# The products with w_down in three column pieces of 342, 342 and 340 instead of two of 512

## The chip, the core and the metric

The kernel runs on one core of a Trainium2 chip. The metric is the time of one execution in microseconds (us); three runs of the kernel before gave 2617.18, 2617.27 and 2620.52, so the median is 2617.27 us. A trace of one further execution of the same kernel goes with them. Its engines are TensorE (PE: matmuls; PEld: the loads of the stationary operand, which the trace lists apart), VectorE (DVE), ScalarE (ACT), GpSimd (POOL) and SyncE (SP, which issues the DMAs).

## The reference, cut to what matters

Two transformer blocks follow one another on 1024 tokens of 1024 features, all in float32. The first mixes a gated delta rule with a dilated attention, the second a gated unit with a depthwise convolution of width 31. Each ends in a feed-forward stage, and only these two stages are touched. In them `x` is (1024, 1024), `D_FF` is 2816, and `w_ff2` has 4096 rows:

```
u = causal_dwconv(h @ w_up, ffn_conv_w)
gate, up = u[..., :D_FF], u[..., D_FF:]
x = x + (jax.nn.silu(gate) * up) @ w_down          # first block
...
f = jnp.square(jax.nn.relu(jnp.einsum('bsd,df->bsf', h, w_ff1[l])))
x = x + jnp.einsum('bsf,fd->bsd', f, w_ff2[l])      # second block
```

## The kernel before

Every product is made from float32 operands that are split in a high and a low part of a 4-byte format. `mm3` (L283) makes one product of a 128x128 stationary tile and a moving tile as three matmuls into the same accumulator: low by high, high by low, high by high. Each matmul has its own weight load. All of them go through `mm` and have line L281 in the profile.

`ffn` (L1545) makes a feed-forward stage. For each of its row blocks f of 128 hidden features (22 in the first block, 32 in the second) it makes the up products (tile `ps_up`, 512 columns), and after each second f it calls `down` for the two blocks before. `down` (L1563) goes over the 8 token tiles, and for each it runs `tile` (L1550): two halves of the 1024 output columns, each one PSUM tile `ps_dn` of 512 columns, into which 2 x 3 matmuls are added up (4 x 3 for the last four token tiles of a stage, where the last two pairs of f are taken together). The stationary operand is the hidden activations of the token tile (`g.hi`, `g.lo`), the moving operand is a slice of a row block of w_down (`w.hi`, `w.lo`, 1024 columns each in one buffer of 2048 words). After each half VectorE adds the PSUM tile to the residual `x[i]` (a tensor_tensor, L315, recorded by `evac`, L343). PSUM has 8 tiles of 512 columns (L357).

The order of all instructions is made on the host: `Weaver.run` (L137) keeps tasks with priorities and models when each engine becomes free (`cost`, L124). A matmul counts 0.417 ns a column there, a tensor_tensor 75 ns and 1.042 ns an element. The task that the model finds due issues its next step, and each engine then executes its own instructions in exactly that order. So a changed count of steps can change the order of work elsewhere.

After a token tile's last piece in the last `down` of the first stage, `last1` (L1749) normalises it, stores it and prepares it for the second block; when four tiles are through, `norm_half` (L549) transposes them (tile `ps_tr`). Then `in2` (L1865) begins: its products (`ps_vg`) feed a convolution of width 31 (`conv31`, L1801) over four groups of channels m = 0 to 3. It runs as chains of VectorE scalar_tensor_tensor steps (L327), 128x512 for m = 0 and 128x1024 for the others. Only for m = 3 the first three taps are matmuls (tile c31, shown as `ps_c`), which ScalarE brings into SBUF before VectorE goes on with that group. `conv_ln` (L1840) normalises each finished half group with two further PE steps (`ps_ct`, `ps_cb`). `block2` (L1915) has its products `ps_v` (256 columns) and `ps_u` in between, and the product `ps_out` of the second block waits for all of it. The second feed-forward stage ends the program: `last2` (L2052) normalises and stores each token tile.

Of the kernel before, what the change touches and what calls it, by code (L numbers as in the profile page):

```python
# [14 lines left out]
ALU = mybir.AluOpType  # L15
# [4 lines left out]
H = 512  # L20
D = 1024
# [52 lines left out]
def after(*evs):  # L74
    def cond():
        return max((e.t for e in evs), default=0.0) if all(e.done for e in evs) else -1.0
    return cond
# [181 lines left out]
class Prog(Weaver):  # L259
# [1285 lines left out]
    def ffn(self, x, h, hev, nf, np_, up, mid, tail, last):  # L1545

        G = {}
        self.gT = Ring([self.unit() for _ in range(2)])

        def tile(i, last_, todo):  # L1550
            kk = [(g, w) for ws, gs in todo for g, w in zip(gs, ws)]
            ts = slice(i * P, (i + 1) * P)
            for n in (0, H):
                ps = self.psum("dn")
                for q, (g, w) in enumerate(kk):
                    self.mm3(ps, g.hi[:, ts], g.lo[:, ts], w.hi[:, 0, n:n + H], w.lo[:, 0, n:n + H], q == 0, q == len(kk) - 1)
                e = self.evac("DVE", lambda xs=x[i][:, n:n + H], ps=ps: self.tt(xs, xs, ps, ALU.add))
                if n and last_:
                    last(i, after(e))
                self.hold = True  # L1560
                yield "PE"

        def down(*fs):  # L1563

            took = []
            for f0 in fs:
                ws = yield from self.pops(self.wq, 2)
                took.append((ws, [G.pop(f) for f in (f0, f0 + 1)]))
                gs = took[-1][1]
                yield "PE", after(*[g.ev[0] for g in gs])  # L1570
                if len(fs) == 1:
                    yield "PE", after(*[g.ev[1] for g in gs])
                if f0 == nf - 2:
                    tail()
                for i in range(4 if len(fs) > 1 else NT):
                    yield from tile(i, f0 == nf - 2, took[-1:])
            if len(fs) > 1:
                yield "PE", after(*[g.ev[1] for _, gs in took for g in gs])
                for i in range(4, NT):
                    yield from tile(i, True, took)  # L1580
            for ws, gs in took:
                for w in ws:
                    self.put(self.W, w)
                for g in gs:
                    self.put(self.gT, g.slot)
                    if len(fs) > 1:
                        s = yield from self.gT.get("PE")
                        s.buf.give()

        for f in range(nf):  # L1590
            G[f] = g = Slot(None)
            g.ev = [Ev(), Ev()]
        first = 2 // np_
        ws = yield from self.pops(self.wq, 2)
        for hf in range(2):
            yield "PE", after(*hev[hf])
            for q in range(2):
                f, p = q // np_, q % np_
                ps = self.psum("up")
                self.gemm_fm(ps, ws[q], 0, h[hf])  # L1600
                yield from up(f, p, hf, ps, G[f])
                if hf:
                    self.put(self.W, ws[q])
                self.hold = True
                yield "PE"
        for f in range(first, nf):
            g = G[f]
            if np_ == 2 and f == nf - 1:
                ws = yield from self.pops(self.wq, 2)
                for hf in range(2):  # L1610
                    for p, w in enumerate(ws):
                        ps = self.psum("up")
                        self.gemm_fm(ps, w, 0, h[hf])
                        yield from up(f, p, hf, ps, g)
                        if hf:
                            self.put(self.W, w)
                        self.hold = True
                        yield "PE"
                    for p in h[hf]:
                        p.give()  # L1620
                    if not hf:
                        for _ in range(2):
                            self.put(self.gT, self.unit())
                break
            for p in range(np_):
                w = yield from self.pop(self.wq)
                for hf in range(2):
                    ps = self.psum("up")
                    self.gemm_fm(ps, w, 0, h[hf])
                    yield from up(f, p, hf, ps, g)  # L1630
                    self.hold = True
                    yield "PE"
                self.put(self.W, w)
                if p == 0 and f % 2 == 0 and f < nf - 2:
                    yield from down(f - 2)
        else:
            for hb in h:
                for p in hb:
                    p.give()
                self.put(self.gT, self.unit())  # L1640
        mid()
        yield from down(nf - 4, nf - 2)
# [473 lines left out]
```

## Time and profile before

| | |
|---|---|
| median of three runs | 2617.27 us |
| profiled execution, time / span of its instructions | 2619.11 us / 2617.3 us |
| PE busy | 2540.3 us, 97% of the span |
| PE weight loads busy | 2180.4 us, 83% |
| VectorE / ScalarE busy | 1370.7 us, 52% / 807.9 us, 31% |
| mean granted clock of TensorE | 0.987 of 2.4 GHz |

A row of the list of groups reads: line, engine, operation, output tile <- inputs, shape, count, then busy time in us, mean ns of one instruction, and the idle time of the engine just before the group with what ended it. Matmuls overlap in the pipeline, so the mean duration of one (389 ns) is longer than the distance from one start to the next; that distance is read from a timeline, where a run of equal instructions stands in one row with its start, its length and its count. The difference of two rows' starts, divided by the count of the first, is the time that one of its matmuls takes from the sequence.

### The profile page before, as it was taken

What the parts mean: (1) busy time and instruction counts of PE and PEld (TensorE: products, weight loads), DVE (VectorE), ACT (ScalarE), POOL (GpSimd) and SP (SyncE); (2) the same over time, 40 slices, a digit from 0 to 9 for tenths busy, and PEclk for the clock granted to TensorE, in tenths of its full rate; (3) what the DMA queues carried; (4) which work ended last, traced back from release to release, by engine and by line L of the source; (5) the groups of instructions that cost most, each with busy time, mean ns of one, the idle gap of its engine ahead of it and who ended that gap; (6) DMA issues with size and microseconds to landing.
All of it is one profiled execution on the core that took longest, in us unless ns stands there. A gap on an engine that the chain in (4) does not pass through costs nothing.

```text
span 2617.3 us, 31361 instructions
## 1 busy us (share of the span) xinstructions
PE 2540.3 (97%) x13001; PEld 2180.4 (83%) x13001; DVE 1370.7 (52%) x1868; ACT 807.9 (31%) x1306; POOL 121.1 (5%) x245
## 2 busy tenths in 40 slices
PE   7999999988989999999999999989999999999998
PEld 6888999988978888888888888877788888888887
DVE  5441343454654555555555567969554444444444
ACT  5322443453541422222222235253232121212122
POOL 1010000000000000000000001050000000000000
PEclk9999999998989999999999999999999999999999
DMA  5232222232441111111111113102211111111111
GB/s 189 71 104 85 84 67 62 80 80 69 106 130 57 41 49 49 49 50 50 49 50 49 50 66 101 61 9 90 71 41 57 41 57 41 57 41 57 41 49 65
DMA packets 175164, 170.80 MB, mean 65 GB/s; under 512 B 25985, under 2 KB 148254, under 8 KB 175022
## 3 DMA queue, kind: packets, MB, share of 16 engines
q1 hardware_dynamic: 175022, 168.80, 21.2%
q8 instruction: 102, 1.67, 0.3%
q14 instruction: 40, 0.33, 0.0%
HBM read 145.50 MB, written 23.23 MB: 64 GB/s over the span
## 4 chain that ended last, share of the span: by engine, by line
PE 61%; issue 28%; DVE 4%; ACT 3%; DMA 2%; POOL 2%; SPq 0%; POOLq 0%; ACTq 0%; DVEq 0%
PE ps_up L281 18%; PE ps_dn L281 9%; PE ps_in L281 5%; PE ps_out L281 5%; PE ps_vg L281 3%; PE ps_dil L281 3%; PE ps_T L281 2%; ACT arF L311 2%; PE ps_S L281 2%; PE ps_z L281 2%; PE ps_O L281 2%; PE ps_dv L281 2%; DVE arF L327 2%; PE ps_pU L281 1%; PE ps_G L281 1%
## 5 line engine op out<-in xcount | busy, mean ns | idle before, releaser
L281 PE MATMUL ps_up<-arR 128*128 128x512 f32 x3648 | 831.5, 389 | 0.0
L281 PEld LDWEIGHTS ps_up<-arR 128*128 128x128 f32 x3648 | 684.5, 188 | 142.1
L315 DVE TENSOR_TENSOR arR<-arF,arR 128x1024 fp32r<-128x1024 f32 (+3 forms) x283 | 347.6, 1236 | 610.0 <-ACT arR L311 609.5
L281 PE MATMUL ps_dn<-arR 128*128 128x512 f32 x2592 | 591.8, 389 | 0.0
L311 ACT ACTIVATE arR<-arF 128x1024 fp32r<-128x1024 f32 (+3 forms) x297 | 311.2, 1071 | 852.3 <-PE ps_dn L281 394.3
L281 PEld LDWEIGHTS ps_dn<-arR 128*128 128x128 f32 x2592 | 486.4, 188 | 101.0
L315 DVE TENSOR_TENSOR arF<-arF,ps_dn 128x512 f32<-128x512 f32 x416 | 279.6, 684 | 183.2 <-PE ps_dn L281 183.2
L327 DVE SCALAR_TENSOR_TENSOR arF<-arF,pcol 128x1024 f32<-128x1024 f32 (+1 forms) x276 | 311.4, 1149 | 22.5 <-ACT arF L311 17.5
L311 ACT ACTIVATE arF<-arF 128x1024 f32<-128x1024 f32 (+3 forms) x158 | 134.8, 860 | 272.5 <-DVE arF L315 138.5
L281 PE MATMUL ps_out<-arR 128*128 128x512 f32 x768 | 182.2, 398 | 2.7 <-DVE arR L315 2.7
L281 PEld LDWEIGHTS ps_out<-arR 128*128 128x128 f32 x768 | 146.7, 192 | 34.4 <-DVE arR L315 3.7
L311 ACT ACTIVATE arF<-ps_up 128x512 f32<-128x512 f32 x152 | 89.5, 589 | 187.0 <-PE ps_up L281 187.0
L281 PE MATMUL ps_in<-arR 128*128 128x512 f32 x576 | 137.7, 399 | 0.0
L281 PEld LDWEIGHTS ps_in<-arR 128*128 128x128 f32 x576 | 109.4, 192 | 23.9
L315 DVE TENSOR_TENSOR arF<-arF 128x1024 f32<-128x1024 f32 (+4 forms) x91 | 89.1, 979 | 28.8 <-ACT arF L311 14.8
L281 PE MATMUL ps_dil<-arR 128*128 128x512 f32 x384 | 97.4, 403 | 0.0
L281 PE MATMUL ps_vg<-arR 128*128 128x512 f32 x384 | 88.3, 390 | 0.0
L281 PEld LDWEIGHTS ps_vg<-arR 128*128 128x128 f32 x384 | 71.8, 188 | 14.8
L281 PEld LDWEIGHTS ps_dil<-arR 128*128 128x128 f32 x384 | 71.7, 192 | 14.2
L281 PE MATMUL ps_O<-arF 128*128 128x128 f32 (+2 forms) x384 | 69.9, 328 | 12.2 <-ACT arF L311 6.8
L315 DVE TENSOR_TENSOR arF<-ps_G,csq 128x512 f32<-128x512 f32 x48 | 33.1, 690 | 90.8 <-PE ps_G L281 90.8
L315 DVE TENSOR_TENSOR arF<-arF,ps_out 128x512 f32<-128x512 f32 x64 | 43.5, 683 | 62.1 <-PE ps_out L281 62.1
(185 smaller groups left out, 2037.2 us busy)
## 6 DMA issues: line engine op xcount, KB each, us to landing
arF<-in_w_ff_dram SPq DMA_DIRECT2D x64, 512.0 KB
arF<-in_w_up_dram SPq DMA_DIRECT2D x44, 512.0 KB
arF<-in_w_in_dram SPq DMA_DIRECT2D x12, 1024.0 KB
arF<-in_w_down_dram SPq DMA_DIRECT2D x22, 512.0 KB
arF<-in_x_dram SPq DMA_DIRECT2D x16, 512.0 KB
arF<-in_w_out_dram SPq DMA_DIRECT2D x16, 512.0 KB
arF<-in_w_in_dram SPq DMA_DIRECT2D x16, 512.0 KB
arF<-kd SPq DMA_DIRECT2D x28, 256.0 KB
```

Of the source, the lines that this page charges most:

```text
L281: self.nc.tensor.matmul(out, lhsT, rhs, start=start, stop=stop, **kw)
L311: self.nc.scalar.activation(out, in_, func, **kw)
L315: self.nc.vector.tensor_tensor(out, a, b, op)
L327: self.nc.vector.scalar_tensor_tensor(out, a, s, b, op0, op1)
```

## The change

The two halves of 512 columns in `tile` become three pieces, columns 0 to 341, 342 to 683 and 684 to 1023. Each piece takes one PSUM tile, of which the first 342 or 340 columns are used, its own matmuls on the same stationary operands, and its own VectorE addition into `x`. The step that follows a token tile's last piece is issued after the third piece.

```
-            for n in (0, H):
-                ps = self.psum("dn")
+            for n, m in ((0, 342), (342, 684), (684, D)):
+                ps = self.psum("dn")[:, :m - n]
                 for q, (g, w) in enumerate(kk):
-                    self.mm3(ps, g.hi[:, ts], g.lo[:, ts], w.hi[:, 0, n:n + H], w.lo[:, 0, n:n + H], q == 0, q == len(kk) - 1)
-                e = self.evac("DVE", lambda xs=x[i][:, n:n + H], ps=ps: self.tt(xs, xs, ps, ALU.add))
-                if n and last_:
+                    self.mm3(ps, g.hi[:, ts], g.lo[:, ts], w.hi[:, 0, n:m], w.lo[:, 0, n:m], q == 0, q == len(kk) - 1)
+                e = self.evac("DVE", lambda xs=x[i][:, n:m], ps=ps: self.tt(xs, xs, ps, ALU.add))
+                if m == D and last_:
                     last(i, after(e))
```

The order of instructions is the same up to the first `ps_dn`. In both stages the row of 96 matmuls of 512 columns of a `down` becomes 144 of 342 and 340. At the end of the first stage the transposes move among the pieces too. On PE, from the end of the last `down` of the first stage, before:

```order
L281 MATMUL ps_dn<-arR 128x512 x168
L291 MATMUL ps_tr<-csq,arF 128x128 x32
L281 MATMUL ps_dn<-arR 128x512 x24
L281 MATMUL ps_vg<-arR 128x512 x72
L291 MATMUL ps_tr<-csq,arF 128x128 x32
L281 MATMUL ps_vg<-arR 128x512 x192
```

On PE at the same place, now (from the piece of the last token tiles on, where 12 matmuls make one piece):

```order
L281 MATMUL ps_dn<-arR 128x342 x24
L281 MATMUL ps_dn<-arR 128x340 x12
L281 MATMUL ps_dn<-arR 128x342 x12
L291 MATMUL ps_tr<-csq,arF 128x128 x32
L281 MATMUL ps_dn<-arR 128x342 x12
L281 MATMUL ps_dn<-arR 128x340 x12
L281 MATMUL ps_dn<-arR 128x342 x24
L281 MATMUL ps_dn<-arR 128x340 x12
L281 MATMUL ps_vg<-arR 128x512 x48
L291 MATMUL ps_tr<-csq,arF 128x128 x32
L281 MATMUL ps_vg<-arR 128x512 x168
```

The first 32 transposes now stand inside a token tile, and the second 32 have one product `ps_vg` of 24 matmuls fewer ahead of them.

On PE in `block2`, around the matmuls of the convolution's group m = 3 (`ps_c`), before:

```order
L281 MATMUL ps_v<-arR 128x256 x312
L281 MATMUL ps_ct<-csq,arF 128x128 x12
L281 MATMUL ps_c_11730<-arF 128x512 x3
L281 MATMUL ps_v<-arR 128x256 x24
L291 MATMUL ps_cb<-csq,arF 128x128 x4
L281 MATMUL ps_c_11795<-arF 128x512 x3
L291 MATMUL ps_cb<-csq,arF 128x128 x8
```

On PE at the same place, now:

```order
L281 MATMUL ps_v<-arR 128x256 x240
L281 MATMUL ps_ct<-csq,arF 128x128 x4
L281 MATMUL ps_v<-arR 128x256 x48
L291 MATMUL ps_cb<-csq,arF 128x128 x4
L281 MATMUL ps_ct<-csq,arF 128x128 x8
L281 MATMUL ps_v<-arR 128x256 x24
L281 MATMUL ps_c_12432<-arF 128x512 x3
L281 MATMUL ps_v<-arR 128x256 x24
L291 MATMUL ps_cb<-csq,arF 128x128 x8
L281 MATMUL ps_c_12502<-arF 128x512 x3
```

The second `ps_c` stands behind the same 336 matmuls of `ps_v` as before, but behind all twelve `ps_cb` instead of four.

On VectorE in the same stretch, from the first step of group m = 2, with the semaphores that a step waits for, before:

```order
L323 TENSOR_SCALAR arF<-arF,pcol 128x1024 [waits DVE_49,Pool_49]
L327 SCALAR_TENSOR_TENSOR arF<-arF,pcol 128x1024 [waits DVE_49] x12
L327 SCALAR_TENSOR_TENSOR arF<-arF,pcol 128x1024 [waits Activation_49,Pool_49]
L327 SCALAR_TENSOR_TENSOR arF<-arF,pcol 128x1024 [waits DVE_49] x3
L315 TENSOR_TENSOR arR<-arF,arR 128x1024 [waits DMAHW7_49,Activation_49]
```

On VectorE at the same place, now:

```order
L323 TENSOR_SCALAR arF<-arF,pcol 128x1024 [waits DVE_49,Pool_49]
L327 SCALAR_TENSOR_TENSOR arF<-arF,pcol 128x1024 [waits DVE_49] x18
L327 SCALAR_TENSOR_TENSOR arF<-arF,pcol 128x1024 [waits Activation_49,Pool_49]
L327 SCALAR_TENSOR_TENSOR arF<-arF,pcol 128x1024 [waits DVE_49] x3
L315 TENSOR_TENSOR arR<-arF,arR 128x1024 [waits DMAHW7_49,Activation_49]
```

The step that waits for ScalarE is the first tap of group m = 3 on VectorE; 18 taps of group m = 2 stand ahead of it instead of 12.

## Rows read from the trace of the kernel before

**Rows 1.** The page: busy time, share and instructions; clock in tenths, 40 slices.

```profile
PE 2540.3 (97%) x13001; PEld 2180.4 (83%) x13001; DVE 1370.7 (52%) x1868; ACT 807.9 (31%) x1306; POOL 121.1 (5%) x245
PEclk9999999998989999999999999999999999999999
```

**Rows 2.** Stretches: length, busy time by engine (instructions), granted clock, DMA share, GB/s.

```profile
920.00:1590.00 670.00, 670.00 (x2974) 555.34 (x2973) 371.21 (x409) 170.54 (x220) 13.57 (x63) 1.00 0.17 52
1590.00:1910.00 320.00, 304.31 (x1598) 258.63 (x1597) 245.59 (x280) 122.45 (x271) 51.89 (x71) 0.98 0.19 61
1910.00:2609.00 699.00, 699.00 (x3103) 579.30 (x3101) 328.23 (x391) 144.31 (x183) 6.73 (x18) 1.00 0.16 49
```

**Rows 3.** The costliest groups: busy us, mean ns | idle before, releaser.

```profile
L281 PE MATMUL ps_dn<-arR 128*128 128x512 f32 x2592 | 591.8, 389 | 0.0
L281 PEld LDWEIGHTS ps_dn<-arR 128*128 128x128 f32 x2592 | 486.4, 188 | 101.0
L281 PE MATMUL ps_G<-arF 128*128 128x128 f32 x384 | 50.9, 278 | 0.0
```

**Rows 4.** Timeline of PE, first down of stage one: start us, length us, instructions.

```profile
923.11 21.92 PE L281 MATMUL ps_dn<-arR 128*128 128x512 f32 x96
944.87 43.68 PE L281 MATMUL ps_up<-arR 128*128 128x512 f32 x192
988.39 21.92 PE L281 MATMUL ps_dn<-arR 128*128 128x512 f32 x96
```

**Rows 5.** Timeline of PE, a run of 256 columns and the row behind it.

```profile
1683.67 37.59 PE L281 MATMUL ps_v<-arR 128*128 128x256 f32 x312
1721.10 2.84 PE L281 MATMUL ps_ct<-csq,arF 128*128 128x128 f32 x24
```

**Rows 6.** Timeline of PE, a run of 260 columns and the row behind it.

```profile
177.10 46.14 PE L281 MATMUL ps_z<-arR 128*128 128x260 f32 x384
223.08 4.33 PE L281 MATMUL ps_dil<-arR 128*128 128x512 f32 x18
```

**Rows 7.** Timeline of PE, an early run of 512 columns and the row behind it.

```profile
129.08 16.88 PE L281 MATMUL ps_in<-arR 128*128 128x512 f32 x72
145.80 1.84 PE L281 MATMUL ps_ss<-ones,arF 128*128 128x1 f32 x16
```

**Rows 8.** Timeline of PE, a run of 128 columns in plain float32.

```profile
304.74 1.95 PE L281 MATMUL ps_G<-arF 128*128 128x128 f32 x16
```

**Rows 9.** VectorE groups that read PSUM, 512 and 256 columns.

```profile
L315 DVE TENSOR_TENSOR arF<-arF,ps_dn 128x512 f32<-128x512 f32 x416 | 279.6, 684 | 183.2 <-PE ps_dn L281 183.2
L315 DVE TENSOR_TENSOR arF<-ps_T,band 128x256 f32<-128x256 f32 x8 | 3.4, 424 | 4.7 <-PE ps_T L281 3.9 <-ACT arF L311 0.7
```

**Rows 10.** PE's waits between 1590 and 1910: us in total, times, longest.

```profile
PE ps_ct L281 <- DVE arF L327: 7.8, 2, 5.6
PE ps_c L281 <- ACT arF L311: 6.4, 1, 6.4
PE ps_out L281 <- DVE arR L315: 0.7, 1, 0.7
PE ps_cb L291 <- ACT arF L311: 0.5, 1, 0.5
PE ps_u L281 <- DVE arR L315: 0.4, 1, 0.4
```

**Rows 11.** Timeline of VectorE around the first tap of group m = 3.

```profile
1717.11 15.81 DVE L327 SCALAR_TENSOR_TENSOR arF<-arF,pcol 128x1024 f32<-128x1024 f32 x12
1750.41 4.87 DVE L327 SCALAR_TENSOR_TENSOR arF<-arF,pcol 128x1024 f32<-128x1024 f32 x4 [17.50 <-ACT arF L311]
```

**Rows 12.** Timeline of ScalarE: a reload of its function table, between 1740 and 1750.

```profile
1743.78 1.28 ACT L311 ACT_TABLE_LOAD   x1
```

**Rows 13.** Timeline at the end: the last addition and the last step on VectorE.

```profile
2609.42 0.69 DVE L315 TENSOR_TENSOR arF<-arF,ps_dn 128x512 f32<-128x512 f32 x1 [0.84 <-PE ps_dn L281]
2612.28 1.28 DVE L327 SCALAR_TENSOR_TENSOR arF<-arF,r 128x1024 f32<-128x1024 f32 x1 [2.17 <-POOL r L370]
```

## The prediction

> **What bounds the kernel now.** I read the page's busy times first, then stretches of the program, then the timeline of TensorE inside the stages that change. The page shows PE busy for 97% of the span at nearly full clock [rows 1]. Cut into stretches, both feed-forward stages are busy throughout: 670.00 of 670.00 us and 699.00 of 699.00 us, at a granted clock of 1.00, the 2.4 GHz level [rows 2]. VectorE has 371.21 and 328.23 us of work there, so it is half free. The group of the down products has 0.0 us of idle time before it [rows 3], and VectorE waits 183.2 us for these products, not the other way round [rows 9]. So in these stages the time is the number of matmuls times the distance from one start to the next, and nothing else. What lies between the stages is different: from 1590 to 1910 us PE is idle for 15.7 of 320 us, waiting for VectorE and ScalarE [rows 2, 10].
>
> **What one matmul costs.** A run of 96 down products starts at 923.11 and the next run at 944.87, so each takes 21.76 us / 96 = 226.67 ns; the up products give 43.52 / 192 = 226.67 ns [rows 4]. 512 columns at 2.4 GHz are 213.33 ns, so 13.3 ns lie on top. A run of 256 columns of the same format takes (1721.10 - 1683.67) us / 312 = 119.97 ns [rows 5], against 106.67 ns of columns: 13.3 ns again. The two rows give a straight line: (226.67 - 119.97) / 256 = 0.4168 ns a column, which is the 2.4 GHz clock, and 13.3 ns for each matmul whatever its width.
>
> **The matmuls that the change adds.** It turns each pair of matmuls of 512 columns into three of 342, 342 and 340. The columns stay 1024, the matmuls (and the loads ahead of them) go from 2592 to 3888. From the row of 256 columns, 342 cost 119.97 + 86 x 0.4168 = 155.8 ns and 340 cost 155.0 ns. Three are 466.6 ns, two of 512 were 453.3 ns, so a trio costs 13.3 ns more. There are 2592 / 2 = 1296 of them: 1296 x 13.26 ns = +17.2 us, all on PE, which has no slack in the stages.
>
> That value lies between bounds. The cheapest row is that of 260 columns: (223.08 - 177.10) us / 384 = 119.74 ns, 11.4 ns above its columns [rows 6]. With 11.4 ns, 342 and 340 cost 153.9 and 153.1 ns, a trio 460.9 ns, and the sum is +9.8 us. The dearest row is an early run of 512 columns: (145.80 - 129.08) us / 72 = 232.2 ns, 5.6 ns above the down products at the same width [rows 7]. These two early runs read other buffers, laid out at other addresses, and it seems that a few ns either way come from where operands start. In the changed kernel the second and third pieces start at columns 342 and 684 of the buffer instead of at 512, so this can matter. With 5.6 ns on two pieces of three a trio costs 24.4 ns more, +31.6 us; on all three +38.8 us. I take the middle, because the 256 and 512 rows at 13.3 ns come from buffers of the same kind as those of w_down, and both stand between and around the new widths.
>
> **The loads.** Each matmul has a load, and 1296 more are issued. A record of a load lasts 188 ns [rows 3], longer than 155 ns, but records overlap: a run of 16 matmuls of 128 columns in plain float32 lasts 1.95 us, the last of them 278 ns of that [rows 3, 8], so there are (1950 - 278) / 15 = 111.5 ns from start to start, with a load for each. So loads can follow each other at 111.5 ns and fit under the 142 ns of 340 columns. I cost them at nothing; the cover would be gone only below 268 columns (111.5 ns at 2.4 GHz).
>
> **VectorE's additions.** They go from 416 to 624. An addition takes 684 ns at 512 columns and an operation of the same kind 424 ns at 256 [rows 9], 1.016 ns a column, so 511 ns at 341. Per token tile that is 1.53 us instead of 1.37 us, under at least 2.8 us of matmuls. In all 624 x 511 - 416 x 684 = +34 us of VectorE work, spread over stages in which it waits 183.2 us for these very tiles. Cost on the path: nothing. The eight PSUM tiles hold one piece each for a shorter time than before. At the end of the program the last addition is shorter by 684 - 511 = 0.17 us, and the chain behind it (square, power, scaling, store) is unchanged [rows 13]: -0.2 us.
>
> **The order between the stages.** The scheduler's model counts a matmul by its columns alone, so it sees no longer stages, but VectorE's steps differ, and the order between 1590 and 1910 us is another one. Two things pull in opposite directions. VectorE stood still for 17.50 us ahead of the first tap of group m = 3, after 12 taps of group m = 2 that took 15.81 us [rows 11]; now 18 taps stand ahead, so 6 x 1.28 = 7.7 us of its work move into that stall. Against this, what it waits for comes later: ahead of the second `ps_c`'s copy ScalarE now has one more normalisation and two more reloads of its table, 1.28 us each [rows 12], and PE has all the `ps_cb` ahead of it, each waiting for ScalarE. I estimate 3 to 5 us from these rows. PE feels the difference through its waits for `ps_ct` and `ps_c`, 14.2 us of the 15.8 us [rows 10]. Bounds: a gain of at most these 15.8 us, more likely up to 4 us, a loss of up to 6 us where the new, earlier `ps_ct` stands in front of products that could run. I take 0.
>
> **Sum.** 17.2 - 0.2 + 0 = +17.0 us. Against the profiled execution's own 2619.11 us (its span is 2617.3 us, 1.8 us lie around it) that is 2636.1 us; the profiled execution was 1.8 us above the median of the runs, so from 2617.27 us the forecast is 2634.3 us, 0.65% slower.
>
> **Rivals.**
> *No fixed part.* If what a matmul takes beyond its columns grew with them, 226.67 / 512 = 0.4427 ns a column, 1024 columns would cost 453.3 ns in any number of pieces and the sum would be -0.2 us: 2617.1 us. The row of 256 columns speaks against it: it would be 113.3 ns and is 119.97 ns [rows 5]. For it speaks only that 256 and 260 columns take nearly the same [rows 5, 6], as if a floor other than the matmul's own cost held both; but loads go at 111.5 ns [rows 8], so they are not that floor. The Trainium skill (TensorE: Matmul & The Clock Gate, Part 1, "Wait — 56ns, not 53.3ns?") gives about 2.5 ns as the fixed cost of a warm matmul; by it the sum would be some 1296 x 2.5 ns = +3.2 us, an estimate from that page. The trace of this kernel disagrees by a factor of five.
> *The stage between pays it back.* This is the case that ends not slower. If the 7.7 us of VectorE's taps that move into the stall pull all later convolution steps forward, PE's waits for `ps_ct` and `ps_c` can vanish. With all 15.8 us gone the sum is +1.2 us: 2618.5 us, no change. It decides from the point where at most some 4 us of the 15.8 us remain. Against it: PE's wait for `ps_c` hangs on ScalarE's chain and not on VectorE, and that chain gets longer.
> *Starts off a boundary are dear.* 5.6 ns more on the two displaced pieces: 2617.3 + 31.4 = 2648.7 us. The early 512 row speaks for it [rows 7]; the 260 row, whose second half starts off a multiple of 256 columns too, against it [rows 6].
> *Cheaper, as at 260 columns.* 2617.3 + 9.6 = 2626.9 us.
> *Loads bind after all.* 3 x 188 - 453.3 = 110.7 ns a trio, +143 us: 2760 us. The 256 and 260 rows, at 120 ns with a load each, rule it out almost fully.
>
> **How the numbers follow.** Forecast 0.70; cheaper 0.11; dearer starts 0.09; the stage between pays it back 0.05; no fixed part or a small one 0.04; loads 0.01. The range goes from 2624 us (the cheaper case with 3 us gained between the stages) to 2646 us (the forecast with 6 us lost there and 6 us of dearer starts); it leaves out the two cases without change, the loads and most of the dearer starts. A difference below 0.2%, some 5 us, is about what a measurement of this kernel cannot tell from no change. Slower takes the forecast, the cheaper and the dearer cases and the loads, 0.91; the cases around zero give 0.08 within and 0.01 faster.
>
> **What would show it.** In the profile of the changed kernel a `down` of 144 matmuls should take 48 x 466.6 ns = 22.4 us from its start to the next `ps_up` (21.76 us before). 21.8 us would mean no fixed part, 22.1 us the cheaper case, above 22.8 us dearer starts, and the pieces of 342 columns that start at 0 and at 342 would then differ. The idle time of `ps_dn` on PE should stay 0.0. The sum of PE's waits between the last `ps_dn` of the first stage and the first `ps_up` of the second should stay within 10 and 22 us; below 4 us the second rival holds. A wait of PE for VectorE's additions inside a stage would make the whole reading wrong.

## The result, and the profile after

The kernel with three pieces takes 2645.41 us (median of four runs, 2644.61 to 2646.19). The kernel before, on the same chip and its four runs taken together, takes 2617.22 us (2613.17 to 2620.52). The ratio is 1.0108, with a 95% interval of 1.0091 to 1.0126, so the changed kernel is 28.2 us slower, 1.1%. The forecast was +17.0 us and 2634.3 us; the time lies 0.6 us below the top of the range.

The page of the changed kernel, busy time with share and instructions by engine, then the granted clock in tenths over 40 slices:

```profile
PE 2559.9 (97%) x14297; PEld 2301.3 (87%) x14297; DVE 1396.4 (53%) x2076; ACT 809.8 (31%) x1308; POOL 120.4 (5%) x245
PEclk9999999998989999999999999989999999999999
```

It holds 14297 - 13001 = 1296 matmuls more than [rows 1], as many loads more and 208 VectorE additions more. PE is as full as before and one slice between the stages is colder. The three stretches of the program, with the columns of [rows 2]:

```profile
920.00:1610.00 690.00, 690.00 (x3556) 614.31 (x3555) 386.52 (x498) 179.36 (x232) 20.23 (x73) 1.00 0.17 53
1610.00:1935.00 325.00, 304.64 (x1594) 258.99 (x1593) 245.11 (x279) 120.04 (x267) 45.52 (x65) 0.97 0.18 58
1935.00:2637.00 702.00, 700.97 (x3829) 642.47 (x3827) 341.03 (x511) 141.38 (x178) 5.84 (x14) 1.00 0.16 49
```

Inside the feed-forward stages PE has no gap to speak of, at a granted clock of 1.00. The groups of the down products, with the columns of [rows 3, 9]:

```profile
L281 PE MATMUL ps_dn<-arR 128*128 128x342 f32 (+1 forms) x3888 | 610.5, 318 | 0.0
L281 PEld LDWEIGHTS ps_dn<-arR 128*128 128x128 f32 x3888 | 607.9, 188 | 2.0
L315 DVE TENSOR_TENSOR arF<-arF,ps_dn 128x342 f32<-128x342 f32 (+1 forms) x624 | 305.6, 507 | 171.5 <-PE ps_dn L281 170.7
```

The idle time of the matmuls is still 0.0, and VectorE still waits for PE. An addition takes 507 ns (worked out beforehand: 511 ns). The timeline of PE, the first `down` of the first stage and one of the second (start, length, instructions; a row is named after its first form and holds the pieces of 340 columns too):

```profile
924.95 22.62 PE L281 MATMUL ps_dn<-arR 128*128 128x342 f32 x144
947.40 43.68 PE L281 MATMUL ps_up<-arR 128*128 128x512 f32 x192
...
2027.70 21.92 PE L281 MATMUL ps_up<-arR 128*128 128x512 f32 x96
2049.46 22.61 PE L281 MATMUL ps_dn<-arR 128*128 128x342 f32 x144
2071.91 21.92 PE L281 MATMUL ps_up<-arR 128*128 128x512 f32 x96
```

From the start of a `down` to the next `ps_up` it is 947.40 - 924.95 = 22.45 us, and 2071.91 - 2049.46 = 22.45 us. Before it was 21.76 us [rows 4]. The up products beside it still take 21.76 us for 96.

To see where the 28.2 us come from, I cut both profiled executions at five points that every kernel here has: the first `ps_up`, the first `ps_dn`, the first `ps_vg`, the first `ps_up` of the second stage, and the last `ps_dn`. The numbers are differences of the starts of these matmuls in each trace, in us.

| | before the first `ps_up` | first feed-forward (`ps_dn` to `ps_vg`) | between (`ps_vg` to `ps_up`) | second feed-forward (`ps_up` to last `ps_dn`) | tail |
|---|---|---|---|---|---|
| before | 865.20 | 667.19 | 319.08 | 699.61 | 8.34 |
| after | 867.04 | 674.92 | 325.01 | 710.78 | 7.90 |
| difference | +1.84 | +7.73 | +5.93 | +11.17 | -0.44 |

The code ahead of the first `ps_up` is the same in both. In the profiled executions of all kernels of this study that stretch lies between 861.4 and 868.4 us, so I take the 1.84 us as scatter, and so much of the spread of the runs. The other stretches repeat to 0.1 us wherever the code in them is the same, except that between the stages it is 318.1 to 319.4 us. In these two executions the change therefore costs **18.9 us in the two feed-forward stages and 5.9 us between them**, and gives 0.4 us back in the tail. The rest, up to 28.2 us, is the first stretch and the profiled execution of before, which was 1.9 us above its median.

PE's waits in the changed kernel between the stages (us in total, times, longest), and VectorE's timeline around the first tap of group m = 3:

```profile
PE ps_cb L291 <- ACT arF L311: 14.8, 3, 6.8
PE ps_vg L281 <- DVE arR L315: 2.8, 2, 2.0
PE ps_ct L281 <- DVE arF L327: 1.8, 1, 1.8
PE ps_out L281 <- DVE arR L315: 0.8, 1, 0.8
```

```profile
1722.51 23.11 DVE L327 SCALAR_TENSOR_TENSOR arF<-arF,pcol 128x1024 f32<-128x1024 f32 x18
1767.17 4.88 DVE L327 SCALAR_TENSOR_TENSOR arF<-arF,pcol 128x1024 f32<-128x1024 f32 x4 [21.55 <-ACT arF L311]
```

The waits for `ps_ct` and `ps_c`, 14.2 us before [rows 10], have shrunk to 1.8 us. In their place stand 14.8 us for `ps_cb` (0.5 us before) and 2.8 us for `ps_vg` (none before): 20.2 us in all instead of 15.8 us. Place by place in the two timelines, much of this is a change of name. The first wait for `ps_cb`, 6.8 us, stands where the kernel before waits 6.4 us for `ps_c`, and the third, 5.2 us, where it waits 5.6 us for `ps_ct`. What is new are the 2.8 us for `ps_vg`, among the transposes that moved, and 2.8 us for the second `ps_cb`. VectorE's stall, 17.50 us behind 12 taps [rows 11], is 21.55 us behind 18 taps.

### The profile page after: what moved, and what is told of

The parts are those of the page before. It is cut to its first block, busy times and chain, and to the rows that moved or that the text cites. A ratio compares the mean times of both kernels' runs of the same rounds, so it can differ in the third digit from the quotient of the medians.

```text
span 2643.6 us, 34163 instructions
## 1 busy us (share of the span) xinstructions
PE 2559.9 (97%) x14297; PEld 2301.3 (87%) x14297; DVE 1396.4 (53%) x2076; ACT 809.8 (31%) x1308; POOL 120.4 (5%) x245
## 3 DMA queue, kind: packets, MB, share of 16 engines
q8 instruction: 112, 1.84, 0.3%
## 4 chain that ended last, share of the span: by engine, by line
PE 63%; issue 28%; DVE 3%; ACT 2%; DMA 2%; POOL 1%; SPq 0%; POOLq 0%; ACTq 0%; DVEq 0%
PE ps_up L281 18%; PE ps_dn L281 9%; PE ps_out L281 6%; PE ps_in L281 5%; PE ps_vg L281 3%; PE ps_dil L281 3%; PE ps_T L281 2%; PE ps_u L281 2%; PE ps_S L281 2%; PE ps_z L281 2%; PE ps_dv L281 2%; PE ps_O L281 2%; ACT arF L311 1%; PE ps_pU L281 1%; PE ps_G L281 1%
## 5 line engine op out<-in xcount | busy, mean ns | idle before, releaser
L281 PE MATMUL ps_dn<-arR 128*128 128x342 f32 (+1 forms) x3888 | 610.5, 318 | 0.0
L281 PEld LDWEIGHTS ps_dn<-arR 128*128 128x128 f32 x3888 | 607.9, 188 | 2.0
L315 DVE TENSOR_TENSOR arF<-arF,ps_dn 128x342 f32<-128x342 f32 (+1 forms) x624 | 305.6, 507 | 171.5 <-PE ps_dn L281 170.7
L315 DVE TENSOR_TENSOR arF<-arF 128x1024 f32<-128x1024 f32 (+4 forms) x91 | 89.1, 979 | 27.9 <-ACT arF L311 14.8
L281 PEld LDWEIGHTS ps_vg<-arR 128*128 128x128 f32 x384 | 71.6, 188 | 18.1 <-issue 3.4
L281 PEld LDWEIGHTS ps_dil<-arR 128*128 128x128 f32 x384 | 71.4, 192 | 14.2
```

The costliest lines, as they stand in the source:

```text
L281: self.nc.tensor.matmul(out, lhsT, rhs, start=start, stop=stop, **kw)
L315: self.nc.vector.tensor_tensor(out, a, b, op)
```

## The experiments

### What a narrower matmul costs

These kernels change the second feed-forward stage alone, so what lies in front of it is the kernel before. Each is read from the start of the first `ps_up` of that stage to the start of its last `ps_dn` (699.61 us before), which holds 768 sets of matmuls on the same stationary operand. A stage change of 0.77 us is 1 ns a set.

**Three pieces in the second stage alone.**

```
-            for n in (0, H):
+            for n, m in ((0, 342), (342, 684), (684, D)) if nf == NFT2 else ((0, H), (H, D)):
...
```

The lines left out here and in the next cuts are those of the change.

> Pieces of 342, 342 and 340 in the second feed-forward stage alone. Theory: 768 x 14.6 ns = +11.2 us there, from the first up product to the last down product 710.8 us instead of 699.6 us, and -0.4 us behind it: about 2628.0 us; the three pieces cost 158.0, 156.6 and 153.2 ns a matmul. Rival (the cost came with the first stage's order): below 2622 us.

Measured: 2627.82 us against 2616.28 us, ratio 1.0049 (1.0034 to 1.0064). The stage takes 710.77 us, +11.16 us, as in the changed kernel; the first stage stays at 667.19 us and the stretch between at 319.09 us. So the cost in this stage is its own: 11.16 us / 768 = 14.5 ns a trio.

**Four pieces of 256 columns** (`(0, 256), (256, H), (H, 768), (768, D)` in the same line).

> Second stage alone, in four pieces of 256 columns, twice the matmuls of before. Theory of 13.3 ns for each matmul, and flat distances because the width never changes inside a down: 120.0 ns a matmul, 768 x 26.7 ns = +20.5 us, 720.1 us from the first up product to the last down product, about 2637 us. Rival (the cost comes from mixing widths, not from the number of matmuls): +0 to 5 us.

Measured: 2639.67 us against 2616.98 us, ratio 1.0088 (1.0071 to 1.0105). One `down` on PE's timeline:

```profile
2033.58 23.20 PE L281 MATMUL ps_dn<-arR 128*128 128x256 f32 x192
2056.61 21.95 PE L281 MATMUL ps_up<-arR 128*128 128x512 f32 x96
```

That is 23.03 us / 192 = 119.95 ns a matmul, of which the columns are 106.67 ns. The stage takes 720.47 us, +20.86 us. So the fixed part is 13.3 ns for `w_down` itself too, at starts 0, 256, 512 and 768, with a load for each, and a set of four has no other cost.

**The additions alone**: matmuls of 512 columns, but two VectorE additions of 256 columns for each.

```
+                if nf == NFT2:
+                    for c in (0, 256):
+                        e = self.evac("DVE", lambda xs=x[i][:, n + c:n + c + 256], pc=ps[:, c:c + 256]: self.tt(xs, xs, pc, ALU.add))
```

> Matmuls in two halves of 512 as before; in the second stage VectorE adds each half in two operations of 256 columns, so it has 4 additions a token tile instead of 2. Theory (additions lie beside the matmuls): 699.6 us from the first up product to the last down product as before, the end shorter by some 0.3 us, 2617 us. Rival (more additions cost PE or the PSUM tiles something): more than 700.5 us there.

Measured: 2622.60 us in one run, and the stage takes 699.61 us, to the hundredth that of before. The additions cost this stage nothing. The run itself is 5.6 us above the median of before, and nothing that the edit touches shows it: its first stretch, with the same code, took 868.39 us, 3.2 us more than in the trace of before, and the tail 8.40 us, so the 0.3 us that I had expected there did not come.

**Other widths that start on multiples of 64**: 384, 320, 320 and 512, 256, 256.

> Second stage alone, in pieces of 384, 320 and 320 columns, so that all starts and widths are multiples of 64 columns. Theory that a matmul pays 13.3 ns whatever its width and that the further 1.3 ns of a trio came from starts or widths off a boundary: 173.3, 146.7 and 146.7 ns flat, 768 x 13.33 ns = +10.2 us, about 2627.2 us, and every distance the same to the ns. Rival (the 1.3 ns has nothing to do with addresses): distances scattered over some 8 ns as with 342 and 340, +11.2 us.

> Second stage alone, in pieces of 512, 256 and 256 columns: as many matmuls as with 342, 342 and 340. Theory (13.3 ns a matmul, whatever the split): 226.7, 120.0 and 120.0 ns, +10.2 us, 709.8 us from the first up product to the last down product. Where a change of width costs by itself, as in the row of 384 columns at 177.9 instead of 173.3 ns, the first matmuls of each piece deviate and it is 710 to 713 us.

Measured: 2632.11 us against 2616.28 us for the first, ratio 1.006 (1.0045 to 1.0075), and 2628.96 us in one run for the second. The stages take 712.78 and 712.41 us, +13.17 and +12.80 us, more than with 342, 342, 340. For the first kernel neither sum came true (+10.2 and +11.2 us); the second lies in the 710 to 713 us that I gave for changes of width. One `down` of each:

```profile
2031.36 22.72 PE L281 MATMUL ps_dn<-arR 128*128 128x384 f32 x144
2053.92 21.95 PE L281 MATMUL ps_up<-arR 128*128 128x512 f32 x96
```

```profile
2031.61 22.70 PE L281 MATMUL ps_dn<-arR 128*128 128x512 f32 x144
2054.15 21.95 PE L281 MATMUL ps_up<-arR 128*128 128x512 f32 x96
```

These are 22.56 and 22.54 us, against 22.40 us with 13.3 ns for each of the 144. Both kernels start all their pieces on multiples of 64 columns, so such starts alone do not make the sets cheap. The trace's starts, matmul by matmul, show where it goes. In the second kernel the six matmuls of 512 columns that follow narrower ones are 233, 236, 228, 232, 231 and 227 ns apart, and then the first two of 256 columns 113 and 119 ns, all others 120 ns. It is the same in every token tile from the second on, to 1 ns. Six are a whole piece there; where a piece has twelve, in the last four token tiles of the stage, the second six are 226 or 227 ns apart.

**The narrower piece first**: 340, 342, 342.

> Second stage alone, pieces in the order 340, 342, 342 columns: the cyclic order of widths is the same as with 342, 342, 340, but every piece starts at another column (0, 340, 682). Theory (the distance of two matmuls hangs on the sequence of widths): 153.2 ns for the pieces of 340, 158.0 and 156.6 ns for those of 342 that follow, 710.8 us from the first up product to the last down product. Rival (it hangs on where a piece starts, with the piece at column 0 the dearest): the piece of 340 columns at column 0 becomes the dearest and the others change.

Measured: 2635.43 us in one run, the stage 713.36 us, +13.75 us. The piece of 340 columns takes 155.3 ns on the mean and those of 342 columns 157.5 ns. Neither expectation came true. The piece at column 0 is not the dearest. But with the same widths in the same cyclic order the sum is not that of 342, 342, 340 either, and the pattern is another one: from the third token tile of a `down` on, the six matmuls of 340 columns are 158, 159, 149, 154, 155 and 158 ns apart, where they were 155, 151, 156, 151, 156 and 150 ns. So the sequence of widths does not settle it; where the pieces start, or their place in the token tile, takes part.

**One width, twice.** The last two runs take away the change of width within a set: 342, 342, 342, where the third piece starts at 682, computes two columns a second time and adds the other 340, and 320, 320, 320, which leaves out the last 64 columns.

```
+            for n, m in ((0, 342), (342, 684), (682, D)) if nf == NFT2 else ((0, H), (H, D)):
...
+                c = 2 if n == 682 else 0
+                e = self.evac("DVE", lambda xs=x[i][:, n + c:m], ps=ps[:, c:]: self.tt(xs, xs, ps, ALU.add))
```

> Stage two alone in three pieces, all of the same width 342: columns 0 to 341, 342 to 683 and 682 to 1023; the third computes two columns twice and adds only its last 340. The time from the first ps_up of stage two to the last ps_dn is the reading (699.61 us with two pieces of 512, 710.77 us with 342/342/340). Theory A (a change of width between neighbouring pieces disturbs the even distances): with one width everything is even at 342 / 2.4 + 13.3 = 155.8 ns, a trio 467.4 ns, 768 trios x 14.1 ns = +10.8 us, 710.4 us, and every matmul of ps_dn lies within 1 ns of 155.8 ns. Theory B (the width 342 itself, or starts off a multiple of 64 columns, makes the distances uneven): they still scatter by some 10 ns in a fixed pattern, and the sum may lie on either side of 710.4 us by up to 2 us.

> Stage two alone in three pieces of 320 columns; the last 64 of the 1024 output columns are left out, so 1/16 of the down products of this stage is not computed. The reading is again first ps_up to last ps_dn of stage two. Theory A (only a change of width disturbs): all even at 320 / 2.4 + 13.3 = 146.7 ns, a trio 440.0 ns against 453.3 ns, 768 x -13.3 ns = -10.2 us, 689.4 us. Theory B (a width that is no multiple of 256 is uneven by itself): the distances scatter as at 342 columns, and the sum is above 689.4 us by 0.5 us or more.

Measured: 2631.31 and 2606.08 us in one run each, against 2618.55 us in one run of before, the stages 712.21 and 689.72 us. One `down` of each, 342 first:

```profile
2033.99 22.70 PE L281 MATMUL ps_dn<-arR 128*128 128x342 f32 x144
2056.53 21.93 PE L281 MATMUL ps_up<-arR 128*128 128x512 f32 x96
```

```profile
2028.48 21.28 PE L281 MATMUL ps_dn<-arR 128*128 128x320 f32 x144
2049.59 21.95 PE L281 MATMUL ps_up<-arR 128*128 128x512 f32 x96
```

With 320 columns a matmul takes 21.11 us / 144 = 146.6 ns, 13.3 ns above its columns, and 2262 of 2303 distances are 146 or 147 ns. With 342 it takes 22.54 us / 144 = 156.5 ns, 14.0 ns above its columns, and the distances go from 151 to 165 ns in a pattern that is the same in every `down`, to 1 or 2 ns. So theory A holds for 320 columns and theory B for 342: that width is uneven with no change of width near it. And 320 columns, which are even alone, are not when 384 stand beside them. Both effects exist.

Theory B left open whether the width or the starts make 342 uneven, and this trace says more. In the last four token tiles of the stage a piece is a run of twelve matmuls. In each of them the second six of the piece at column 342 are 153 or 154 ns apart, those at column 0 from 151 to 165 ns and those at column 682 from 156 to 160 ns. The width is the same in all three, and so are the stationary operands. So the start takes part, but not as a rule of starts off a boundary: the piece at column 342 becomes the even one.

Width is not the whole of it in the kernel before either. Its early run of 512 columns [rows 7], at a granted clock of 1.00, is a steady 232, 234 or 235, and 226 or 227 ns in turn behind a first distance of 314 ns. Its run of 78 matmuls of 256 columns for `ps_dv`, from 452.44 us, settles at 120, 114, 118, 112, 119 and 117 ns. Both read other buffers than the down products. The table collects the distances from start to start in this stage, in ns, with what lies above the columns at 2.4 GHz.

| pieces | mean distance | above the columns | seen |
|---|---|---|---|
| 512, 512 (before) | 226.67 | 13.3 | 226 or 227 |
| 256 x 4 | 119.96 | 13.3 | 120 (3043 of 3071) |
| 320 x 3 | 146.63 | 13.3 | 146 or 147 |
| 342 x 3 | 156.49 | 14.0 | 151 to 165 |
| 342, 342, 340 | 157.27; 153.22 | 14.8; 11.6 | 151 to 165; 150 to 157 |
| 340, 342, 342 | 155.30; 157.50 | 13.6; 15.0 | 149 to 160; 153 to 165 |
| 384, 320, 320 | 177.87; 145.99 | 17.9; 12.7 | 170 to 185; 140 to 147 |
| 512, 256, 256 | 230.56; 119.40 | 17.2; 12.7 | 226 to 236; 113 to 120 |

### What the order between the stages costs

The order that the host makes for the stretch between the stages changes as soon as the last `down` of the first stage issues three additions a token tile. So I split the change there.

```
+            for n, m in ((0, 342), (342, 684), (684, D)) if nf == NFT and last_ else ((0, H), (H, D)):
```

> Three pieces only for the last addition of each token tile at the end of the first stage (96 pairs of 1296); all else in two halves of 512. The order of instructions between the stages is then that of the changed kernel. Theory (the order costs by itself): 96 x 14.6 ns = +1.4 us of matmuls and +5.9 us from the order between the stages, with PE's waits there near 20 us instead of 15.8 us: about 2624.5 us. Rival (the 5.9 us came from run to run, or from the longer matmuls): +1.4 us, 2618.6 us, waits as before.

Measured: 2623.31 us against 2616.28 us, ratio 1.0029 (1.0018 to 1.0041). These are 96 trios of 1296. They cost 668.34 - 667.19 = 1.15 us in the first stage, and the second stage is at 699.61 us. But the stretch between takes 325.77 us, +6.7 us. Its order is that of the changed kernel, and so are PE's waits there, 21.8 us in all:

```profile
PE ps_cb L291 <- ACT arF L311: 15.1, 3, 6.8
PE ps_vg L281 <- DVE arR L315: 2.8, 2, 2.0
```

The opposite, three pieces everywhere but there:

```
+            for n, m in ((0, H), (H, D)) if nf == NFT and last_ else ((0, 342), (342, 684), (684, D)):
```

> The opposite: three pieces everywhere but for the last addition of each token tile of the first stage. The order between the stages is that of the kernel before. Theory: 1200 x 14.6 ns = +17.5 us of matmuls, -0.4 us at the end, nothing between the stages, waits near 15.8 us: about 2634.3 us. Rival: the stage between is longer whatever the order, 2640 us.

Measured: 2634.42 us against 2616.28 us, ratio 1.0073 (1.0056 to 1.009). The stages cost +6.59 and +11.16 us. The stretch between is at 318.71 us and its waits are those of [rows 10]:

```profile
PE ps_ct L281 <- DVE arF L327: 7.8, 2, 5.6
PE ps_c L281 <- ACT arF L311: 6.4, 1, 6.4
```

The two halves add up: 1.15 + 6.59 = 7.74 us in the first stage (7.73 in the changed kernel), and the whole of the 5.9 us between the stages comes with the changed order, with no matmul of that stretch made longer by the edit. By the medians of the runs the halves are 7.0 and 18.1 us, 25.2 us together, nearer to the 24.4 us of the stretches than to 28.2 us.

I then asked whether the matmuls of group m = 3 and ScalarE's copy of them, for which VectorE stands still, are the cause. In both kernels the three taps went to VectorE.

```
-    KP0, KP1, KP2, KP3 = 0, 0, 0, 3
+    KP0, KP1, KP2, KP3 = 0, 0, 0, 0
```

> The changed kernel, with the first three taps of the convolution's group m = 3 made by VectorE like the others instead of by TensorE and ScalarE, so that VectorE no longer waits for ScalarE there. Theory (the 5.9 us between the stages come from the chain through ScalarE and GpSimd, for which VectorE stands still 21.6 us): that stall goes, three taps more cost 3.8 us of VectorE, PE's waits between the stages fall from 20.2 us to under 12 us, and the stretch from the first ps_vg to the second stage's first ps_up from 325.0 to some 315 us; about 2635 us. Rival (PE's waits come from the order of ps_ct and ps_cb alone): the stretch stays within 3 us of 325 us.

> The kernel before with the same edit. Theory: the 17.5 us stall of VectorE goes, PE's waits fall from 15.8 us to some 8 us, the stretch between the stages from 319.1 us to some 312 us: about 2610 us, a little faster than before. Rival (VectorE's total work sets the end of that stretch and the stall was slack): within 2 us of 319.1 us, or longer by the 3.8 us of the added taps.

Measured: the changed kernel goes to 2639.55 us (ratio to before 1.0084, 1.007 to 1.0097) and its stretch between to 318.63 us, 6.4 us shorter. The kernel before goes to 2632.56 us (ratio 1.005, 1.0036 to 1.0064) and its stretch to 331.08 us, 12.0 us longer, where I had expected it to be shorter. None of the four expectations came true. In the changed kernel PE's waits did not fall under 12 us, they are 21.1 us; the stretch is shorter because PE is busy for 297.53 us in it instead of 304.65 us, without the twelve matmuls of `ps_c`. In the kernel before the waits went from 15.8 to 28.2 us. As the edit reorders the stretch in both kernels, it does not tell what these matmuls cost by themselves; but without them the waits are there all the same. The stall of VectorE is still there in both, now ahead of the next thing that ScalarE gives it (the changed kernel first):

```profile
1732.55 14.43 DVE L327 SCALAR_TENSOR_TENSOR arF<-arF,pcol 128x1024 f32<-128x1024 f32 x12
1768.68 1.22 DVE L315 TENSOR_TENSOR arR<-arF,arR 128x1024 fp32r<-128x1024 f32 x1 [21.69 <-ACT arR L311]
```

```profile
1719.58 15.63 DVE L327 SCALAR_TENSOR_TENSOR arF<-arF,pcol 128x1024 f32<-128x1024 f32 x13
1764.57 1.23 DVE L315 TENSOR_TENSOR arR<-arF,arR 128x1024 fp32r<-128x1024 f32 x1 [29.37 <-ACT arR L311]
```

What holds ScalarE in the second of these shows on GpSimd's timeline, and on PE's, which waits for ScalarE at the same time:

```profile
1719.92 15.34 POOL L368 TENSOR_SCALAR ms<-ss 128x1 f32<-128x1 f32 x1 [0.93 <-ACT arF L311]
1735.34 0.55 POOL L370 TENSOR_TENSOR r<-ms,nhalf 128x1 f32<-128x1 f32 x1
```

```profile
1737.42 4.62 PE L281 MATMUL ps_v<-arR 128*128 128x256 f32 x24 [8.74 <-ACT arF L311]
```

A GpSimd operation on one column, which takes 0.19 us elsewhere, lasts 15.34 us there: from 1719.92 us, 0.3 us after the first of VectorE's 13 taps, to 1735.26 us, 0.05 us after the last. Lengths on GpSimd are rough in the profile, but ScalarE's own timeline has the same gap, 16.36 us for GpSimd's `mr`, which follows the two steps above:

```profile
1736.19 0.81 ACT L311 ACTIVATE arF<-arF,mr,r 128x512 f32<-128x512 f32 x1 [16.36 <-POOL mr L335]
```

ScalarE's normalisation waits for GpSimd, PE's `ps_v` for ScalarE. The same can be read, smaller, in the changed kernel, first under the 18 taps, then behind their end at 1745.62 us:

```profile
1731.22 1.59 POOL L370 TENSOR_TENSOR r<-ms,nhalf 128x1 f32<-128x1 f32 x1
1736.51 2.07 POOL L370 TENSOR_TENSOR brs<-ms,nhalf 128x4 f32<-128x4 f32 x1
...
1746.87 0.55 POOL L370 TENSOR_TENSOR r<-ms,nhalf 128x1 f32<-128x1 f32 x1
...
1752.65 1.02 POOL L370 TENSOR_TENSOR brs<-ms,nhalf 128x4 f32<-128x4 f32 x1
```

Each of these small steps takes two to three times as long while VectorE runs taps; another, `nm`, takes 6.59 us under the first of them and 0.27 us behind the last. And here PE waits for the end of such a chain (GpSimd's `brs`, then ScalarE), in the changed kernel:

```profile
1739.03 1.25 PE L291 MATMUL ps_cb<-csq,arF 128*128 128x128 f32 x4 [6.81 <-ACT arF L311]
...
1755.40 2.27 PE L291 MATMUL ps_cb<-csq,arF 128*128 128x128 f32 x8 [2.76 <-ACT arF L311]
```

That GpSimd is slowed under the taps is shown in these traces. That this is what the 5.9 us come from is not shown. The kernel before has the same thing under its own taps:

```profile
1710.36 6.77 POOL L1934 TENSOR_SCALAR nm<-ab 128x1 f32<-128x1 f32 x1 [47.13 <-ACT arF L311]
1718.53 1.59 POOL L370 TENSOR_TENSOR r<-ms,nhalf 128x1 f32<-128x1 f32 x1
```

The longer run of taps may keep GpSimd slow for longer, but how much of the 5.9 us that makes was not measured by a run of its own: the order of PE's and ScalarE's steps changed with it. The second wait for `ps_cb` above lies 7 to 10 us behind the end of the taps. What is shown is the account on PE: 4.4 us more of waiting and 1.3 us more of work. PE is busy for 304.65 us between the first `ps_vg` and the second stage, against 303.39 us, for about as many instructions. The clock has a part in it. From 1740 to 1760 us, behind the first wait for `ps_cb`, the granted clock of the changed kernel is 0.76; from 1730 to 1750 us, behind its wait for `ps_c`, that of the kernel before is 0.86.

## Why the prediction was right, and where it was off

**What bounds the stages: right.** PE is full in both, at a clock of 1.00, and its waits for VectorE's additions inside a stage stay at 0.0. Loads and additions cost nothing, as said. Four pieces of 256 columns with their loads show the one, the split additions the other.

**The fixed part: right in kind.** It is 13.3 ns a matmul, and the run of four pieces of 256 columns gave +20.86 us against 20.5 us worked out with it. The rival without a fixed part, which had this kernel at 2617.1 us, and the one in which loads bind are out.

**The trio: mis-sized by a tenth.** The step says that 342 columns take 155.8 ns and 340 take 155.0 ns. They take 157.27 and 153.22 ns, and a trio costs 14.6 ns more than two of 512 where I had 13.26: (7.73 + 11.17) us / 1296. That is +18.9 us instead of +17.2 us, a `down` of 22.45 us instead of 22.4 us. The straight line was drawn through two runs that are even. The row of 260 columns should have warned me. I took its mean, 119.74 ns, as a cheap fixed part of 11.4 ns; its single distances in the trace of before go from 114 to 125 ns, while those of 512 columns are all 226 or 227 ns. It was not a cheaper matmul but an uneven one, and so are 342 and 340. The row of 512 columns that I took for the dearest [rows 7] is uneven as well, from 226 to 235 ns, and its mean holds a first distance of 314 ns.

**That displaced starts are dearer: fell as it was priced.** "Above 22.8 us dearer starts" did not come. The pieces at 0 and at 342 do differ, which was named as its sign, but the other way round: 158.0 ns at column 0 and 156.5 ns at 342. Pieces that start at 320 and 640 are even, and the sets of 384 and 512 that start on multiples of 64 are dearer than the change. But the guess behind it, that a few ns come from where operands start, is not refuted. With one width in all pieces the one at column 342 runs evenly and the others do not, and the order 340, 342, 342 has another sum. Width, the width that ran just before, and the start take part, and by what rule stays open.

**The order between the stages: the step that failed.** "I take 0" was +5.9 us, at the upper end of the bounds of -4 to +6 us. I had both halves of the second rival's mechanism in hand. The waits for `ps_ct` and `ps_c` did go, 12.4 us of 14.2 us, as it had it. But the `ps_cb` steps, which I named only as something that stands ahead of the second `ps_c`, took 14.3 us more, and `ps_vg` 2.8 us. And I booked six more taps ahead of VectorE's stall as 7.7 us gained. The stall grew from 17.50 to 21.55 us instead. The loss that I did name, a later `ps_c` behind one more normalisation, reloads and all the `ps_cb`, at an estimate of 3 to 5 us, is the side that came. That the chain runs through GpSimd, which the taps slow down, I had not seen; it may add to the stall, which no run shows by itself. PE's waits, 20.2 us, are inside the 10 to 22 us that I had asked for.

**The tail: right.** 8.34 us became 7.90 us. In all traces it is 7.9 to 8.1 us behind narrower last pieces and 8.1 to 8.4 us behind 512 columns, so the -0.2 us fit.

**The sum.** +18.9 + 5.9 - 0.4 = +24.4 us from the change, against +17.0 us. The other 3.8 us up to 28.2 us lie in the first stretch, whose code is the same (1.8 us), and in the 1.9 us by which the profiled execution of before was above its median while that of after was at its own. As far as these traces show, neither belongs to the change. That the time is still inside the range owes something to luck: the lost order used up the whole allowance for it, and 0.6 us were left.

## What to carry to other kernels

Where TensorE is full, cutting the same columns into more matmuls costs a fixed time for each, which two rows of different widths in the trace give; before such a line is used for a width in between, look at the single distances of a row, since a plausible mean can hide an uneven run. A change in the number of steps at the seam of two stages can reorder everything behind it, so run that seam alone, and its opposite: here 96 of 1296 trios carried the whole cost of the order. Do not count VectorE work that moves into a stall as a gain before you know which engines the awaited chain runs through.

## What the runs showed of the hardware

**Even and uneven widths.** Down products of 256, 320 or 512 columns, with a load for each matmul and one width throughout, are even to 1 ns but for the first few of a `down`, at 13.3 ns above the columns. Runs of 260, 342 and 340 columns are not: they scatter over 7 to 14 ns. For 342 and 340 columns it is a pattern that repeats to 1 or 2 ns from `down` to `down`. The width alone does not decide: products early in the program that read other buffers run from 226 to 235 ns at 512 columns and from 112 to 120 ns at 256. Behind narrower matmuls the next wider ones take up to 9 ns more (236 ns for 512 columns) for about six matmuls, and behind wider ones the next narrower one up to 7 ns less (113 ns for 256). The mechanism stays open. The additions are excluded by their own run. Starts off a multiple of 64 columns are excluded as the only cause, since 342 columns are uneven at column 0 and settle to even at column 342. What the addresses of the buffers do was not tested.

**GpSimd under VectorE's taps.** A one-column GpSimd operation that takes 0.19 us otherwise took 15.34 us under 13 back-to-back scalar_tensor_tensor operations of VectorE, and others 1.59 us instead of 0.55 us. The Trainium skill (SBUF — State Buffer, "Who interferes with whom") says that a VectorE instruction with two inputs in SBUF contends with a GpSimd instruction that reads SBUF, because VectorE's second input comes through a read interface that the two share. The trace agrees: a tap reads the input and the running sum, both in SBUF, and GpSimd was free again 0.05 us after the last tap. What the page's rule alone does not tell is whether GpSimd gets in between two taps. In the changed kernel it did, in 0.3 to 2.1 us a step but for one of 6.59 us, and in the kernel with 13 taps it did not until all were through.
